# An engine model that lets only one engine at a time use a PSUM tile, other DMA times in it, and a copy placed ahead of two reads

## The chip, the cores and the metric

The kernel runs on one core of one Trainium2 chip. A core has TensorE (matrix products into PSUM, a memory of eight banks), VectorE and ScalarE (both read and write PSUM and SBUF), GpSimd (SBUF alone), and SyncE, which here issues nearly all DMAs. Each engine works through its own queue in order. The metric is the device time of one execution in microseconds; lower is better.

## The reference

One layer of a streaming encoder on 1024 positions of width 2048, in float32. One input projection (2048 to 6752 columns) feeds two mixers side by side. Cut to what matters here:

```python
u = jnp.einsum('bsd,de->bse', h, w_in[layer])
q, k, v, z_attn, q_idx, k_idx, w_idx, z_ssd, xbc, dt_raw = _split_cols(u, IN_WIDTHS)
...
o_attn = _dsa_attention(q, k, v, q_idx, k_idx, w_idx) * jax.nn.silu(z_attn)
o_ssd = _ssd_mixer(xbc, z_ssd, dt_raw, conv_w[layer], conv_b[layer], dt_bias[layer],
                   a_log[layer], d_skip[layer], ssd_norm_w[layer])
mixed = jnp.concatenate([o_attn, o_ssd.astype(o_attn.dtype)], axis=-1)
sub = jnp.einsum('bse,ed->bsd', mixed, w_out[layer])
h = _layer_norm(DEEPNORM_ALPHA * h + sub, ln_g[layer], ln_b[layer])
```

The attention scores all keys with a small indexer, keeps the best 256 for each query and attends to those. The second mixer is the one that the change edits. It splits the sequence into chunks and computes, for each chunk and group of four heads:

```python
xdt = xs * dt[..., None]
a_cum = jnp.cumsum(dt * a, axis=2)
...
cb = jnp.einsum('bclgn,bcsgn->bclsg', cm, bm)
y_diag = jnp.einsum('bclsg,bclsgr,bcsgrp->bclgrp', cb, lmat, xdt)
decay = jnp.exp(a_cum[:, :, -1:] - a_cum)
states = jnp.einsum('bcsgn,bcsgr,bcsgrp->bcgrpn', bm, decay, xdt)
```

The kernel takes chunks of 128 positions where the reference takes 64; the sum is the same.

## The kernel before

**The products.** A float32 product is made of three products of rounded halves: each operand x is split into a high part (xh, wh: a rounded copy, made by ScalarE) and the rest (xl, wl: x minus the high part, made by VectorE or GpSimd), and TensorE adds hi*hi, hi*lo and lo*hi in one PSUM bank. The input projection runs over column tiles of 128 and halves of 512 positions, the output projection over column blocks of 512; both use sums and differences of blocks (a fast matrix product), whose operands are formed by VectorE or GpSimd and partly stored to DRAM and read again. A piece is one weight block of 128 x 1024 and 24 matmuls. Its weight is loaded to wr, split to wh and wl up to two pieces ahead (WAHEAD, L32; w_split, L950), and used. The first product of a pair stays in its PSUM tile (pj); VectorE then adds a reloaded partial result to it (t_u, L740; t_comb, L769), and only after that TensorE adds the next product to the same tile.

**The order of the work.** Nothing is ordered at run time. When the program is built, a planner (class Flow) emits every instruction in an order that it chooses, with the help of a model of the engines (class Sim, L137). The framework then puts in the semaphores that the data need. The planner walks along the pieces of the two projections; between them it looks at a list of tasks, Python generators in order of priority, and lets a task emit its next instructions when it is ready (L444). A task says at each `yield Need(...)` which engines, free buffers and events it needs next. It is ready when its own last instructions, and the events it names, end by the model no later than about the time at which the engine it names gets to them, and when that engine's queue is not over some 2.65 us ahead of TensorE's. An event of a DMA can be given a margin (late). So a figure of the model that is wrong does not make wrong results: it makes a queue in which an instruction stands before its time, and everything behind it on this engine with it, or one that is asked to work later than it could.

**What the model knows.** Sim.run (L257) gives every instruction a start: the later of its engine's clock and the ends of the earlier instructions on which it depends (deps, L164), plus 70 ns between engines. deps goes over the earlier uses of a tile and takes those that overlap in bytes and partitions, one of the two being a write. Two reads of one tile by two engines therefore do not hold each other up in the model. Durations come from formulas (cost, L205). A DMA (L292) takes a lane of eight, its issuing engine's time, then a place on one modelled transfer queue, and lands a fixed time (LAND, L141) after its transfer.

**The mixer's chunk work.** t_ssd (L1971) runs once for each half of the sequence and group, eight times in all, with four chunks each. It starts when the group's convolved inputs lie in DRAM. For each chunk TensorE transposes three blocks of 128 x 128 into one PSUM bank (tag a, of which there are three); VectorE multiplies the first two, 256 columns, by dt (to xdt) and by ddt (to xdd); ScalarE copies the third to bn. The bank is then free for others. After that come the products of the chunk: the masked cb, the chunk's state from bn and xdd, exponentials on ScalarE, the outputs in PSUM tile o, and a gate that needs a small power from GpSimd.

**Names in the profile.** Buffers are shared between purposes, so u is any 128 x 512 buffer in SBUF (bn, xdt and xdd among them; late in the run also xh and xl), s a larger one, a, pj and o PSUM tiles. Every instruction is recorded on one helper line, L318, so groups are told apart by tile and shape. The copy to bn is `ACT u<-a 128x128`, the two reads are `DVE u<-a,dt` and `DVE u<-a,ddt`.

Of the kernel before, what the change touches and what calls it, by code (L numbers as in the profile page):

```python
# [15 lines left out]
D = 2048  # L16
# [108 lines left out]
def in_psum(x):  # L125
    return "PSUM" in str(x.space)


def in_dram(x):
    return "DRAM" in str(x.space)  # L130


def kind_of(x):
    return str(x.dtype).split(".")[-1]


class Sim:  # L137


    LAT = 70.0  # L140
    LAND = 2500.0  # L141

    def __init__(self):
        self.clk = dict(PE=0.0, V=0.0, A=0.0, G=0.0, SP=0.0, AQ=0.0, D=0.0)
# [19 lines left out]
    def deps(self, outs, ins, eng):  # L164
        at, notes = 0.0, []
        for w, xs in ((False, ins), (True, outs)):
            for x in xs:
                k, name, p0, p1, a, b = self.region(x)
                s = self.slot.get(k)
                if s is None:  # L170
                    s = self.slot[k] = [name, 0.0, []]
                elif s[0] != name:
                    s[:] = [name, max([s[1]] + [e[5][0] for e in s[2]]), []]
                at = max(at, s[1])
                for q0, q1, c, d, wr, end, e in s[2]:
                    if (wr or w) and c < b and a < d and q0 < p1 and p0 < q1:
                        if e == eng == "PE":
                            continue
                        at = max(at, end[0] + (0.0 if e == eng else self.LAT))
                notes.append((s, p0, p1, a, b, w))  # L180
        return at, notes
# [23 lines left out]
    def cost(self, eng, op, outs, ins, kw, n):  # L205

        if eng == "PE":
            n = ins[1].free_size()
            if op == "transpose":
                return 111.0, 290.0  # L210
            if kind_of(ins[1]) == "float32":
                if outs[0].partition_size() <= 64:
                    return 153.0, 300.0
                return 2 * max(n / 2.4 + 4, 100.0) if n > 8 else 226.0, max(n / 2.4, 57.0) + 330
            return n / 2.4 + 14.5 if n > 128 else max(n / 2.4 + 4, 80.0), n / 2.4 + 176
        if eng == "V":
            m = max(x.free_size() for x in [*outs, *ins])
            scalar = any(x.free_size() == 1 for x in ins) and n > 1
            if op in ("max", "match_replace"):
                t = (155 if op == "max" else 261) + 1.042 * m  # L220
            elif op == "bn_stats":
                t = 160 + 1.042 * m
            elif op == "stream_shuffle":
                t = 180 + 1.042 * n
            elif op == "tensor_tensor_scan":
                t = 200 + 2.084 * n
            elif op in ("tensor_scalar", "tensor_copy"):
                t = 145 + (1.042 if in_psum(ins[0]) or in_psum(outs[0]) else 0.64) * n + 45 * scalar
            elif op == "reciprocal":
                t = 145 + 5 * n  # L230
            elif op == "tensor_tensor_reduce":
                return 75 + 1.042 * n, 235 + 1.042 * n
            else:
                t = 145 + 1.042 * n + 60 * (op == "scalar_tensor_tensor" and scalar)
            return t - 80, t
        if eng == "A":
            t = (160 if in_psum(ins[0]) else 190) + 0.853 * n + 85 * (len(ins) > 1) + 100 * (len(ins) > 2)
            return (t - 15, t + 90) if len(outs) > 1 else (t - 97, t)
        if op == "memset":
            t = 90 + n  # L240
        elif op == "tensor_tensor":
            t = 180 + 2.16 * n if n > 8 else 600 + 120 * n
        else:
            t = 230 + 0.88 * n
        return t - 30, t
# [46 lines left out]
    def dma(self, eng, out, in_, kw):  # L292
        q = {"SP": "SP", "A": "AQ", "G": "G"}[eng]
        lanes = self.lanes["G" if q == "G" else "H"]
        at, notes = self.deps([out], [in_], "D")
        start = max(self.clk[q], at, lanes.pop(0))
        issue = 1000.0 if eng == "G" else 350.0
        self.clk[q] = start + issue
        sb = in_ if in_dram(out) else out
        row = max(sb.ap[-1][1] * 4, 64)  # L300
        x = max(start + issue, self.clk["D"])
        self.clk["D"] = x + max(out.size(), in_.size()) * 4 * (1 / 360 + 0.6 / row)
        cell = [self.clk["D"] + self.LAND, start, True]
        lanes.append(cell[0])
        self.note(notes, cell, "D")
        return cell
# [282 lines left out]
class Layer:  # L589
# [1381 lines left out]
    def t_ssd(self, h, g):  # L1971
        fl, nc = self.fl, self.nc
# [7 lines left out]
        for cp in range(2):  # L1980
# [10 lines left out]
            bn, xdt, xdd, hs, ea = [fl.new("u", [P, 2, 256]) for _ in range(5)]  # L1991
# [3 lines left out]
            for k, c in enumerate(cs):  # L1995
                yield Need("P", late=2500.0, a=1)
                b = fl.new("a", [P, 512])
                cl = slice(k * P, (k + 1) * P)
                fl.tr(b[:, 0:128], xs[0][:, cl])
                fl.tr(b[:, 128:256], xs[1][:, cl])  # L2000
                fl.tr(b[:, 256:384], bt[:, cl])
                yield Need("VA")
                fl.tt("V", v4(xdt[:, k]), v4(b[:, 0:256]), bc(sd["dt"], c), ALU.mult)
                fl.tt("V", v4(xdd[:, k]), v4(b[:, 0:256]), bc(sd["ddt"], c), ALU.mult)
                fl.act(bn[:, k, 0:128], b[:, 256:384])
                fl.free(b)
            yield Need("P", a=1)
            b = fl.new("a", [P, 256])
# [15 lines left out]
            for k, c in enumerate(cs):  # L2024
# [4 lines left out]
                b = fl.new("a", [P, 256])  # L2029
# [22 lines left out]
            b = fl.new("a", [P, 2, 2, P])  # L2052
# [311 lines left out]
```

## Time and profile before

| | |
|---|---|
| median of 3 runs | 1685.58 us (1684.43 to 1689.02) |
| the profiled execution | 1687.85 us |
| its span, first to last instruction | 1686.0 us |
| mean granted clock of TensorE | 0.984 |
| share of the span, TensorE / VectorE / ScalarE / GpSimd | 97% / 79% / 59% / 12% |
| DMA | 415.53 MB, 246 GB/s on average |

The span is what the profile's rows cover; 1.85 us of the profiled execution lie around it. A row of a timeline has the start, the length, the engine, the instruction with the tile that it writes and the tiles that it reads, the shape, and in brackets how long the engine stood idle just before it and what ended that. TensorE's clock is granted in steps: after a pause it runs at half speed for some microseconds, and a matmul then takes nearly twice as long while it still counts as busy. The busy share alone therefore hides a part of what a pause costs; the granted clock of a window shows it.

### The profile page before, as it was taken

The page shows a single profiled execution, that of the slowest core. Times are in us where ns is not written, and L with a number is a line of the kernel's source. Part 1 is how long each engine was busy: PE and PEld are TensorE (multiplying, and loading weights), DVE is VectorE, ACT ScalarE, POOL GpSimd, SP SyncE. Part 2 cuts the span into 40 slices and gives each one's busy share as a digit, 9 for nine tenths or more (in the row PEclk, how much of TensorE's full clock was granted, in tenths as well). Part 3 has the DMA queues.
Part 4 walks back from the last instruction along what each step waited for, and adds up shares of the span by engine and source line. Part 5 has one row for each costly group of instructions (what it writes and reads, how often), then busy time and mean ns, then how long its engine had stood idle before and what let it go on. Part 6 is the DMA issues. An engine that isn't in the chain of part 4 may idle for free. (4 is left out here: it accounts for less than half of the span.)

```text
span 1686.0 us, 23971 instructions
## 1 busy us (share of the span) xinstructions
PE 1627.5 (97%) x7996; PEld 1346.7 (80%) x7996; DVE 1325.5 (79%) x2430; ACT 993.4 (59%) x1764; POOL 205.2 (12%) x219
## 2 busy tenths in 40 slices
PE   9999999999998999999999999999898999999997
PEld 7787778888886877888888887888677878788885
DVE  5889998998779866787676679867687686749998
ACT  4555666888886788774433556675746555432330
POOL 0000010000000001211123302221011011000110
PEclk9999999999999999999999999999999999999998
DMA  8177575889778867697586685567787999567754
GB/s 305 60 278 250 197 265 188 285 307 348 266 268 279 295 215 264 198 330 250 191 305 227 197 300 162 182 198 250 286 276 278 304 299 319 176 218 261 232 197 153
DMA packets 193211, 415.53 MB, mean 246 GB/s; under 512 B 19776, under 2 KB 56256, under 8 KB 193088
## 3 DMA queue, kind: packets, MB, share of 16 engines
q1 hardware_dynamic: 192656, 413.61, 71.3%
q8 instruction: 63, 1.03, 0.3%
q14 instruction: 60, 0.49, 0.1%
q10 hardware_dynamic: 432, 0.39, 0.1%
HBM read 309.46 MB, written 104.46 MB: 246 GB/s over the span
## 5 line engine op out<-in xcount | busy, mean ns | idle before, releaser
L318 PE MATMUL pj<-xh,wh 128*128 128x512 f32 (+1 forms) x1496 | 586.8, 392 | 15.7 <-DVE u L318 12.3
L318 PE MATMUL pj<-xh,wl 128*128 128x512 f32 (+1 forms) x1496 | 574.8, 384 | 1.8 <-DVE wl L318 1.7
L318 PE MATMUL pj<-xl,wh 128*128 128x512 f32 (+1 forms) x1496 | 574.3, 384 | 0.2 <-DVE xl L318 0.2
L318 DVE TENSOR_TENSOR wl<-wr,wh 128x1024 fp32r<-128x1024 f32 (+2 forms) x232 | 280.4, 1212 | 181.6 <-ACT wh L318 175.4
L318 PEld LDWEIGHTS pj<-xh,wh 128*128 128x128 f32 x1496 | 284.5, 190 | 70.8 <-issue 15.6
L318 ACT ACTIVATE wh<-wr 128x1024 fp32r<-128x1024 f32 (+2 forms) x242 | 248.3, 1031 | 146.5 <-PE pj L318 112.0
L318 PEld LDWEIGHTS pj<-xh,wl 128*128 128x128 f32 x1496 | 284.1, 190 | 60.4 <-DVE wl L318 4.3
L318 PEld LDWEIGHTS pj<-xl,wh 128*128 128x128 f32 x1496 | 284.7, 190 | 50.5 <-DVE xl L318 0.5
L318 PE MATMUL a<-u,u 128*128 128x512 f32 (+3 forms) x734 | 175.1, 359 | 12.1 <-DVE u L318 5.5
L318 PEld LDWEIGHTS a<-u,u 128*128 128x128 f32 x734 | 121.6, 193 | 47.3 <-DVE s L318 18.1
L318 ACT ACTIVATE u<-a 128x512 fp32r<-128x512 f32 (+4 forms) x114 | 53.6, 484 | 154.8 <-PE a L318 67.2
L318 ACT ACTIVATE u<-s,sm 128x640 bf16<-128x640 int16 (+7 forms) x132 | 129.7, 983 | 24.8 <-DVE sm L318 22.8
L318 DVE TENSOR_TENSOR u<-u,u 128x512 f32<-128x512 f32 (+6 forms) x212 | 137.1, 659 | 7.3 <-DMA u<-zs 2.6
L318 PE MATMUL pj<-wh,xh 128*128 128x512 f32 x310 | 126.5, 408 | 0.2 <-DVE u L318 0.2
L318 PE MATMUL pj<-wh,xl 128*128 128x512 f32 x310 | 121.8, 393 | 0.0
L318 PE MATMUL pj<-wl,xh 128*128 128x512 f32 x310 | 121.6, 392 | 0.0
L318 DVE TENSOR_TENSOR u<-pj,u 128x512 f32<-128x512 f32 (+2 forms) x112 | 74.6, 668 | 56.4 <-PE pj L318 55.8
L318 ACT ACTIVATE a<-a 128x512 f32<-128x512 f32 (+3 forms) x160 | 77.0, 505 | 67.6 <-PE a L318 62.0
L318 ACT ACTIVATE u<-u 128x512 f32<-128x512 f32 (+4 forms) x149 | 81.3, 557 | 55.2 <-DVE u L318 48.3
L318 DVE TENSOR_TENSOR wr<-wr,wr 128x1024 f32<-128x1024 f32 (+1 forms) x75 | 92.4, 1233 | 1.3 <-DMA wr<-wt 0.8
L318 DVE SCALAR_TENSOR_TENSOR u<-cv,cw,u 128x512 f32<-128x512 f32 x96 | 72.8, 764 | 9.0 <-POOL cv L318 5.3
L318 POOL TENSOR_SCALAR s<-s,sm 128x640 f32<-128x640 f32 (+7 forms) x64 | 59.7, 949 | 165.1 <-DVE sm L318 126.0
(259 smaller groups left out, 2209.0 us busy)
## 6 DMA issues: line engine op xcount, KB each, us to landing
wr<-wt SPq DMA_DIRECT2D x187, 512.0 KB, 5.5
u<-u SPq DMA_DIRECT2D x110, 256.0 KB, 4.8
wr<-t SPq DMA_DIRECT2D x44, 512.0 KB, 5.4
u<-wo SPq DMA_DIRECT2D x64, 256.0 KB, 4.6
ts<-u SPq DMA_DIRECT2D x64, 256.0 KB, 3.9
wr<-ts SPq DMA_DIRECT2D x32, 512.0 KB, 4.7
s<-xt SPq DMA_DIRECT2D x24, 512.0 KB, 6.2
t<-wr SPq DMA_DIRECT2D x22, 512.0 KB, 4.4
```

Of the source, the lines that this page charges most:

```text
L318: f(*args, **kw)
```

## The change

Four edits, three in the model and one in the mixer.

- In deps any earlier use of a PSUM tile by another engine counts, whether it reads or writes and whichever bytes it touches.
- The DMA model: the issue takes 450 ns where it took 350; the transfer starts 100 ns after the issue starts, where it started after the whole issue; its length is 8.8 ns and 0.0372 ns a byte for each row, over 16 engines, with rows of the shorter side of the two; a load that repeats its source over many partitions (over 300,000 bytes) has a rate of its own; a load lands 2200 ns after its transfer, a store 1600 (STORED), where both took 2500.
- A float32 matmul into at most 64 partitions occupies TensorE for 111 ns where it took 153.
- In t_ssd the copy to bn is asked for and emitted first, by itself; VectorE's two reads come in a step of their own.

The same instructions are emitted as before. Since the planner goes by the model, the order of nearly everything can differ.

```diff
     LAT = 70.0
-    LAND = 2500.0
+    LAND = 2200.0
+    STORED = 1600.0
...
                 k, name, p0, p1, a, b = self.region(x)
+                bank = in_psum(x)
...
                 for q0, q1, c, d, wr, end, e in s[2]:
-                    if (wr or w) and c < b and a < d and q0 < p1 and p0 < q1:
+                    if bank and e != eng or (wr or w) and c < b and a < d and q0 < p1 and p0 < q1:
                         if e == eng == "PE":
                             continue
                         at = max(at, end[0] + (0.0 if e == eng else self.LAT))
...
                 if outs[0].partition_size() <= 64:
-                    return 153.0, 300.0
+                    return 111.0, 300.0
...
-        issue = 1000.0 if eng == "G" else 350.0
+        issue = 1000.0 if eng == "G" else 450.0
         self.clk[q] = start + issue
-        sb = in_ if in_dram(out) else out
-        row = max(sb.ap[-1][1] * 4, 64)
-        x = max(start + issue, self.clk["D"])
-        self.clk["D"] = x + max(out.size(), in_.size()) * 4 * (1 / 360 + 0.6 / row)
-        cell = [self.clk["D"] + self.LAND, start, True]
+        row = min(max(x.ap[-1][1] * 4, 64) for x in (out, in_))
+        x = max(start + 100.0, self.clk["D"])
+        size = max(out.size(), in_.size()) * 4
+        spread = any(s == 0 and n > 1 for s, n in in_.ap) and size > 300000
+        self.clk["D"] = x + (0.0045 * size if spread else size / row * (8.8 + 0.0372 * row) / 16)
+        cell = [self.clk["D"] + (self.STORED if in_dram(out) else self.LAND), start, True]
...
-                yield Need("VA")
+                yield Need("A")
+                fl.act(bn[:, k, 0:128], b[:, 256:384])
+                yield Need("V")
                 fl.tt("V", v4(xdt[:, k]), v4(b[:, 0:256]), bc(sd["dt"], c), ALU.mult)
                 fl.tt("V", v4(xdd[:, k]), v4(b[:, 0:256]), bc(sd["ddt"], c), ALU.mult)
-                fl.act(bn[:, k, 0:128], b[:, 256:384])
                 fl.free(b)
```

## Prediction

> **What bounds the kernel now.** I read the page first: its engine totals say who is short of time.
>
> ```profile
> span 1686.0 us, 23971 instructions
> PE 1627.5 (97%) x7996; PEld 1346.7 (80%) x7996; DVE 1325.5 (79%) x2430; ACT 993.4 (59%) x1764; POOL 205.2 (12%) x219
> ```
>
> TensorE is busy for 1627.5 of 1686.0 us. The change adds and removes no matmul, so all that it can win lies in the other 58.5 us and in the time that TensorE spends at half clock. Next come busy times by stretch (the columns are length, busy time and instructions of each engine, granted clock, DMA share, GB/s). I cut at 570 and 1460 because the state-space mixer's reads of its transposed tiles lie between, by the view of tile ddt (32 instructions; minimum, median, maximum ns; first and last start):
>
> ```profile
> L318 DVE TENSOR_TENSOR u<-a,ddt x26: 406/414/417, 576.6 to 1457.2; 128x256 f32<-128x256 f32 x26
> L318 DVE TENSOR_TENSOR xh<-a,ddt x6: 411/411/414, 1336.8 to 1415.4; 128x256 f32<-128x256 f32 x6
> ```
>
> ```profile
> core 0: us, PE busy (x) PEld busy (x) DVE busy (x) ACT busy (x) POOL busy (x), PEclk, DMA share, GB/s
> 0.00:570.00 570.00, 552.90 (x2593) 450.12 (x2594) 479.84 (x887) 392.41 (x705) 36.77 (x49) 0.99 0.73 259
> 570.00:1460.00 890.00, 860.70 (x4441) 720.82 (x4441) 656.97 (x1258) 536.80 (x974) 147.05 (x154) 0.98 0.74 249
> 1640.00:1686.00 46.00, 34.03 (x151) 27.84 (x149) 41.01 (x67) 0.00 (x0) 3.92 (x4) 0.90 0.49 160
> ```
>
> Without the mixer (0 to 570) TensorE idles 17.1 us and loses 1% of 570, 5.7 us, to the clock: 22.8 us, or 4.0% of the stretch. With the mixer (570 to 1460) it idles 29.3 us and loses 2% of 890, 17.8 us: 47.1 us, or 5.3%. The clock has two digits, so each loss is good to about half a per cent of its stretch. What ends TensorE's idle time in the mixer's stretch, by the waits (total, times, longest):
>
> ```profile
> PE a L318 <- DVE u L318: 9.3, 8, 2.9
> PE a L318 <- ACT u L318: 6.4, 3, 5.0
> PE pj L318 <- DVE u L318: 6.4, 1, 6.4
> PE a L318 <- POOL sm L318: 2.8, 1, 2.8
> ```
>
> Four stalls (6.4, 5.0, 2.9 and 2.8 us) hold 17.1 of the 29.3 us. No row names a DMA. The bound is thus TensorE plus a handful of jams, and the question is what makes the jams.
>
> **Part 1: two engines on one PSUM tile.** In t_ssd a bank takes three transposes; VectorE reads two of them twice (by dt and by ddt) and ScalarE copies the third. The planner of before lets these readers overlap. The groups by form tell what the chip's program does (busy, mean ns, idle before and what ended it):
>
> ```profile
> L318 ACT ACTIVATE u<-a 128x128 f32<-128x128 f32 x26 | 7.2, 275 | 71.4 <-DVE u L318 43.2 <-issue 9.7 <-DMA wr<-wt 6.4
> L318 ACT ACTIVATE xh<-a 128x128 f32<-128x128 f32 x4 | 1.1, 278 | 18.1 <-DVE u L318 18.1
> ```
>
> ScalarE sat idle 43.2 + 18.1 = 61.3 us before 30 copies of 0.28 us, until VectorE was through. The planner sees none of it: it believes ScalarE free, and queues the next weight split behind the copy. The largest such stall, from the timelines of VectorE, ScalarE and TensorE (start, length, idle before):
>
> ```profile
> 1265.91 2.64 DVE L318 TENSOR_TENSOR u<-u 128x256 f32<-128x256 f32 x1
> 1272.24 0.41 DVE L318 TENSOR_TENSOR u<-a,ddt 128x256 f32<-128x256 f32 x1
> 1272.74 0.28 ACT L318 ACTIVATE u<-a 128x128 f32<-128x128 f32 x1 [7.03 <-DVE u L318]
> 1280.45 1.04 ACT L318 ACTIVATE wh<-wr 128x1024 fp32r<-128x1024 f32 x1
> 1281.52 1.23 DVE L318 TENSOR_TENSOR wl<-wr,wh 128x1024 fp32r<-128x1024 f32 x1 [7.94 <-ACT wh L318]
> 1283.50 0.28 ACT L318 ACTIVATE u<-a 128x128 f32<-128x128 f32 x1 [2.02 <-DVE u L318]
> 1283.83 0.58 PE L318 MATMUL a<-u 128*128 128x128 f32 x1 [5.04 <-ACT u L318]
> ```
>
> It is a ring. ScalarE's copy waits 7.03 us for a VectorE that is behind; ScalarE's later work then starts late, the weight's high half (wh) at 1280.45; VectorE waits 7.94 us for wh; its reads for the second chunk come after that, the second copy after those reads, and TensorE, which needs this copy for the chunk's state, stands 5.04 us. The 2.8 us stall has the same root:
>
> ```profile
> 1242.89 0.28 ACT L318 ACTIVATE u<-a 128x128 f32<-128x128 f32 x1 [3.53 <-DVE sm L318]
> 1243.07 1.06 ACT L318 ACTIVATE wh<-wr 128x1024 fp32r<-128x1024 f32 x1
> 1244.20 2.67 POOL L318 TENSOR_TENSOR wl<-wr,wh 128x1024 fp32r<-128x1024 f32 x1 [70.61 <-ACT wh L318]
> 1247.58 1.22 PE L318 MATMUL a<-c,sm 128*128 128x128 f32 x4 [2.78 <-POOL sm L318]
> ```
>
> The copy waits 3.53 us, wh stands behind it, GpSimd's wl behind wh, and the small power that TensorE needs behind wl. Of the 6.4 us stall only a part is of this kind:
>
> ```profile
> 1191.47 0.28 ACT L318 ACTIVATE u<-a 128x128 f32<-128x128 f32 x1 [1.97 <-DVE u L318]
> 1210.62 0.77 PE L318 MATMUL pj<-xh,wh 128*128 128x512 f32 x1 [6.37 <-DVE u L318]
> ```
>
> A stall also costs clock. The windows around three of them and around the 2.9 us one:
>
> ```profile
> 1202.00:1218.00 16.00, 9.63 (x31) 7.44 (x31) 13.63 (x22) 8.66 (x11) 0.00 (x0) 0.79 0.60 212
> 1241.00:1256.00 15.00, 12.22 (x47) 9.80 (x46) 10.46 (x19) 4.21 (x6) 3.77 (x5) 0.77 0.96 312
> 1276.00:1292.00 16.00, 10.96 (x45) 8.82 (x44) 9.66 (x13) 13.72 (x29) 2.44 (x1) 0.79 0.70 242
> 1010.00:1024.00 14.00, 11.08 (x52) 9.38 (x51) 10.32 (x30) 8.47 (x25) 2.26 (x4) 0.88 0.35 117
> ```
>
> 0.21 of 16 us (0.23 of 15) is 3.4 us of full-speed work each, so these stalls are worth 6.2 to 9.8 us; 0.12 of 14 us is 1.7.
>
> The change makes the planner count any use of a PSUM tile by one engine as a bar to the others, and puts the copy first, so that ScalarE waits for the transposes alone. What it adds: VectorE's two reads now wait for the copy, at most 32 x 0.28 = 9.0 us of VectorE with a free ScalarE; behind them on VectorE stand weight splits and sums, which TensorE needs some pieces later. VectorE has 233 us to spare in this stretch, so I cost this at nothing; without that cover, with ScalarE in a run of its own work, it is the second rival. A yield now lies between copy and reads, and the planner queues the reads only when the copy is due. No DMA or queue is moved by hand, though all of them by the new plan.
>
> Size, from both sides. The two stalls told whole are 5.0 + 2.8 + 2 x 3.4 = 14.6 us; with the 6.4 us stall (9.8 with its clock) and the 2.9 us one (4.6 with its clock) the sum is 29.0 us, and that is the upper end. The lower end is none. But the whole order is drawn again, and a new order has jams of its own. So I take the rate: if the mixer's stretch falls to the 4.0% of the stretch without mixer, its loss goes from 47.1 to 890 x 0.040 = 35.6 us. **The gain is 11.5 us**, near what the two whole stalls give.
>
> The Trainium skill, "PSUM — Partial Sum Buffer", section "PSUM bank collisions raise a hardware error", says that no two engines may use one bank in the same quadrant at once, reads against reads included. By it the turn-taking stays and only the waiter changes; the 61.3 us before the copies agree that readers take turns, and what that could do here is the second rival.
>
> **Part 2: transfer times.** The planner's landing of a 512 KB load (128 rows of 4 KB) falls from 350 + 1533 + 2500 = 4383 ns to 100 + 1289 + 2200 = 3589 ns, that of a 256 KB store (rows of 2 KB) from 350 + 805 + 2500 = 3655 to 100 + 680 + 1600 = 2380. The trace has, from the DMA issues and from the view of tile wt (minimum, median, maximum):
>
> ```profile
> wr<-wt SPq DMA_DIRECT2D x187, 512.0 KB, 5.5
> ts<-u SPq DMA_DIRECT2D x64, 256.0 KB, 3.9
> DMA to landing us min/median/max: 3.1/5.5/10.7
> ```
>
> A load's new figure lies 0.5 us above the minimum and 1.9 under the median; the old one lay 1.1 under it. The planner adds queueing of its own, so some of this is made up, but work behind a load will be queued some 0.8 us earlier against the real landing, and an engine may stand at its head. Such waits are rare now:
>
> ```profile
> ACT u L318 <- DMA wr<-wt: 7.5, 2, 6.4
> ACT u L318 <- DMA u<-q: 6.2, 3, 4.8
> ```
>
> Weights are split two pieces ahead, and a piece is 24 matmuls; the chain of waits has their pace.
>
> ```profile
> 1301.38 15.01 PE pj L318 x66
> ```
>
> At 0.227 us each that is 10.9 us of cover, against 0.8. I cost the part at nothing. Where the cover fails, the price is that of the worst stall outside the mixer, with its window:
>
> ```profile
> 514.88 0.77 PE L318 MATMUL pj<-xh,wh 128*128 128x512 f32 x1 [5.96 <-DVE u L318]
> 505.00:521.00 16.00, 10.04 (x35) 7.76 (x34) 14.59 (x22) 10.80 (x21) 1.24 (x2) 0.79 0.92 346
> ```
>
> 6.0 + 3.4 = 9.4 us each. The lower end is a gain of as much, should the new order miss this very stall. The longer SP issue (450 for 350) and the shorter 64-row matmul (111 for 153) change only the plan and belong to the same bounds.
>
> **Sum.** The tail from 1640 has none of this (ScalarE does nothing there): 0. So -11.5 + 0 + 0. The profiled execution took 1687.85 us (span 1686.0 and 1.85 around it), which gives 1676.4; the median of the runs is 1685.58, 2.3 lower, and from it I get **1674.0 us**.
>
> **The rivals.**
>
> 1. *Every jam of this kind goes and nothing takes its place*: 1685.6 - 29.0 = 1656.6. For it: the rings are plain in the trace. Against: a new order has never been free of jams, since 0 to 570 loses 4.0% with no mixer.
> 2. *The wait only changes sides.* ScalarE stays busy for stretches of 7 us (1272.74 to 1280.45 above, wh behind exponentials); a copy queued behind one holds VectorE's reads, as VectorE held the copy. Loss stays 47.1 us: 1685.6, give or take 5.
> 3. *Slower: optimistic landings.* VectorE adds a reloaded partial product to a PSUM tile, in t_u and t_comb, with no margin for the load; TensorE's next product into that tile waits for the sum. If a landing is later than planned by more than VectorE's queue hides, TensorE stands as at 514.88. Two such stalls eat the gain and three turn it round; with four it is 1685.6 - 11.5 + 4 x 9.4 = 1711.7, with three 1702.3, and if the gain in the mixer is none, one is enough: 1695.0. I price it at 1695.0. The Trainium skill, "DMA: Bandwidth & Descriptors", section "Latency and other measured facts", has HBM's access latency at 0.2 us on average and 2 us at high load; by that rule one fixed landing is too early just when queues are full, and the trace's 3.1 to 10.7 us agrees.
>
> **Chances.** Forecast (a gain of 6 to 20 us) 0.50; rival 1, 0.12; rival 2, 0.20; rival 3, 0.18. Measurement tells about 0.3%, 5 us, from no change. So faster 0.62, same 0.20, slower 0.18. The range must take in the forecast's own 1665 to 1680, no change, and most of rivals 1 and 3: 1657 to 1694.
>
> **What would show it.** Right: idle time before the u<-a and xh<-a copies ended by DVE falls from 61 us to under 15; the waits of PE between 570 and 1460 lose the rows on ACT u and POOL sm; the granted clock there rises; PE busy plus the slower clock in 0 to 570 stay within 6 us of 22.8 lost. Rival 2: VectorE's rows of dt and ddt show idle time ended by ACT u. Rival 3: rows "DVE u <- DMA u<-u" of 10 us and more, and a PE stall of 5 us behind one. Wrong altogether: the copies' waits go, and the loss in the mixer's stretch stays, or 0 to 570 loses more by what the other gains.

## The result, and the profile after

The changed kernel takes 1656.04 us (median of 4 runs, 1655.1 to 1659.73) against 1685.74 us before (1684.43 to 1689.02): 29.7 us less, a ratio of 0.9825 with a 95% interval of 0.9805 to 0.9845. The forecast was 1674.0 with a range of 1657 to 1694: the direction is right, the gain is two and a half times what was forecast, and the time lies 1 us outside the range, at the first rival's 1656.6.

The first lines of the page of after:

```profile
span 1654.3 us, 23979 instructions
## 1 busy us (share of the span) xinstructions
PE 1614.9 (98%) x7996; PEld 1337.3 (81%) x7996; DVE 1323.1 (80%) x2429; ACT 1004.6 (61%) x1772; POOL 204.2 (12%) x220
```

The span is 31.7 us shorter. TensorE's idle time went from 58.5 to 1654.3 - 1614.9 = 39.4 us, 19.1 less; the other 12.6 us are in its busy time, with the same 7996 matmuls. The granted clock was 0.984 in that execution of before and 0.995 in this one, so these 12.6 us are time at half clock, and two fifths of the difference between the two executions is clock. Other executions of before had clocks of 0.983 to 0.991 and took 1679.6 to 1691.3 us, so this share is not the same in each. (One more of them, at 1994.4 us with a clock of 0.751, was in a slower state and is left out everywhere.) Where, by the windows of after (columns as before):

```profile
0.00:570.00 570.00, 556.17 (x2607) 451.92 (x2608) 486.75 (x887) 383.12 (x683) 30.02 (x47) 0.99 0.76 268
570.00:1460.00 890.00, 881.73 (x4621) 740.15 (x4620) 664.98 (x1294) 576.16 (x1035) 154.48 (x160) 1.00 0.73 248
1460.00:1640.00 180.00, 174.60 (x762) 143.51 (x761) 161.07 (x233) 45.28 (x55) 18.75 (x12) 0.99 0.67 224
```

The mixer's stretch idles 8.3 us where it idled 29.3, at a granted clock of 1.00 where it had 0.98. It gets 180 more matmuls done in the same 890 us. The stretch without mixer loses 13.8 us idle and 1% of clock: 19.5 us, where it lost 22.8. What TensorE still waits for in the mixer's stretch, by the waits of after:

```profile
PE a L321 <- DVE sm L321: 2.1, 4, 0.8
PE pj L321 <- ACT u L321: 1.8, 1, 1.8
PE a L321 <- POOL u L321: 1.7, 2, 1.1
PE a L321 <- DVE u L321: 1.5, 3, 0.7
```

All four big stalls are gone; the longest wait in this stretch is 1.8 us. (Behind it, between 1460 and 1640, stands one of 4.7 us on DVE xh.) And the copies, in the groups by form, with the idle time before VectorE's reads of dt from their tile view behind them:

```profile
L321 ACT ACTIVATE u<-a 128x128 f32<-128x128 f32 x32 | 8.5, 269 | 17.9 <-PE a L321 17.7
```

```profile
its engine sat idle before it (us, times) until:
  ACT u L321: 3.7, 1
```

No copy waits for VectorE any more; where ScalarE idles before one, it waits for the transposes. VectorE has paid 3.7 us, in one wait.

This agrees with the ring, but a trace of another order cannot prove it: every queue differs from before. That is what the experiments are for.

### The profile page after: what moved, and what is told of

It is laid out like the page before. It is cut to its first block, busy times and chain, and to the rows that moved or that the text cites. A ratio compares the mean times of both kernels' runs of the same rounds, so it can differ in the third digit from the quotient of the medians.

```text
span 1654.3 us, 23979 instructions
## 1 busy us (share of the span) xinstructions
PE 1614.9 (98%) x7996; PEld 1337.3 (81%) x7996; DVE 1323.1 (80%) x2429; ACT 1004.6 (61%) x1772; POOL 204.2 (12%) x220
## 4 chain that ended last, share of the span: by engine, by line
PE 48%; DVE 13%; ACT 12%; DMA 7%; issue 4%; POOL 0%; SPq 0%; DVEq 0%; ACTq 0%; POOLq 0%
PE pj L321 37%; PE a L321 9%; ACT u L321 8%; DVE u L321 6%; DVE wl L321 3%; PE o L321 2%; ACT wh L321 2%; DMA wr<-wt 2%; DVE xl L321 2%; DVE xh L321 1%; DVE wr L321 1%; ACT s L321 1%; DVE s L321 1%; ACT L321 1%; DMA u<-xn 1%
## 5 line engine op out<-in xcount | busy, mean ns | idle before, releaser
L321 PE MATMUL a<-u,u 128*128 128x512 f32 (+3 forms) x744 | 177.5, 356 | 12.6 <-DVE s L321 5.3
L321 PEld LDWEIGHTS a<-u,u 128*128 128x128 f32 x744 | 120.5, 189 | 52.4 <-DVE s L321 20.4
L321 DVE TENSOR_TENSOR u<-u,u 128x512 f32<-128x512 f32 (+7 forms) x202 | 127.7, 642 | 21.4 <-DMA u<-wo 5.9
L321 ACT ACTIVATE u<-s,sm 128x896 bf16<-128x896 int16 (+7 forms) x132 | 129.5, 982 | 16.6 <-DVE sm L321 14.7
L321 DVE TENSOR_TENSOR wr<-wr,wr 128x1024 f32<-128x1024 f32 (+1 forms) x79 | 97.3, 1233 | 4.1 <-DMA wr<-wt 3.4
L321 POOL TENSOR_SCALAR s<-s,sm 128x640 f32<-128x640 f32 (+7 forms) x64 | 63.2, 1002 | 125.9 <-DVE sm L321 89.2
L321 DVE SCALAR_TENSOR_TENSOR s<-a,wsc,s 128x512 f32<-128x512 f32 (+3 forms) x120 | 73.2, 644 | 6.4 <-ACT a L321 4.3
```

The costliest lines, as they stand in the source:

```text
L321: f(*args, **kw)
```

## The experiments

Three theories: **the ring** (the direction of the wait between the copy and the reads makes the jams), **the draw** (any new order is faster or slower by chance, and this one was lucky), and **the transfer times** (better landings make a better order). Times of before differ a little between the groups of runs, from 1684.3 to 1686.4 us; each ratio is against before on the same chip.

### The wait turned round, all queues kept

The planner of before does not see the wait between two readers. So the copy can be written ahead of the reads in the same step without moving anything in its plan: all five engines get the same instructions in the same order, and only the direction of the wait changes.

```diff
                 yield Need("VA")
+                fl.act(bn[:, k, 0:128], b[:, 256:384])
                 fl.tt("V", v4(xdt[:, k]), v4(b[:, 0:256]), bc(sd["dt"], c), ALU.mult)
                 fl.tt("V", v4(xdd[:, k]), v4(b[:, 0:256]), bc(sd["ddt"], c), ALU.mult)
-                fl.act(bn[:, k, 0:128], b[:, 256:384])
```

> The kernel before with the copy to bn written ahead of VectorE's two reads inside the same step; the planner's model and the order of every engine's queue stay those of before, only the direction of the wait turns. Ring theory (ScalarE's copies waiting for VectorE make the mixer's jams): the idle time before the u<-a and xh<-a copies ended by DVE falls from 61 us to under 5, the 5.0 and 2.8 us stalls go, 1665 to 1673 us. New-order theory (the gain is the draw of another order): nothing moves, 1683 to 1688. Transfer-time theory (the better landings order the work better): 1683 to 1688.

Measured: **1656.65 us**, ratio 0.9834 (0.9813 to 0.9855). The swap, one line moved in the order of before, is worth 28.5 us, nearly the whole gain. The ring theory's range of 1665 to 1673 was missed by 8 us, on the fast side: it priced little more than the two stalls that had been told whole. The page of this run, its copies by form, and its mixer's stretch:

```profile
span 1654.6 us, 23984 instructions
## 1 busy us (share of the span) xinstructions
PE 1614.6 (98%) x7996; PEld 1339.0 (81%) x7996; DVE 1323.3 (80%) x2430; ACT 995.3 (60%) x1764; POOL 205.9 (12%) x219
```

```profile
L318 ACT ACTIVATE u<-a 128x128 f32<-128x128 f32 x26 | 7.0, 267 | 20.3 <-PE a L318 20.1
...
L318 ACT ACTIVATE xh<-a 128x128 f32<-128x128 f32 x4 | 1.1, 272 | 12.2 <-PE a L318 12.2
```

```profile
570.00:1460.00 890.00, 878.42 (x4606) 739.39 (x4605) 675.72 (x1292) 553.94 (x1001) 152.03 (x159) 1.00 0.75 253
```

The idle time that DVE ended, 61.3 us, is gone; TensorE idles 11.6 us instead of 29.3, and the clock stands at 1.00. Here is the pair of copies that made the worst ring before, in this run's timelines of ScalarE and VectorE (in each fence the copies, then the reads):

```profile
1249.24 0.26 ACT L318 ACTIVATE u<-a 128x128 f32<-128x128 f32 x1
...
1258.31 0.26 ACT L318 ACTIVATE u<-a 128x128 f32<-128x128 f32 x1
```

```profile
1255.45 0.41 DVE L318 TENSOR_TENSOR u<-a,dt 128x256 f32<-128x256 f32 x1
...
1259.58 0.42 DVE L318 TENSOR_TENSOR u<-a,dt 128x256 f32<-128x256 f32 x1
```

VectorE is as late as ever: its first read comes 6.2 us after the copy. But nobody waits for it. Neither copy has a bracket, ScalarE goes on to its table and its exponentials, and no TensorE stall follows. Since TensorE's queue is the same in both kernels, the very matmuls that stood 2.92, 2.78, 5.04 and 2.25 us in before can be looked up here. They have no bracket (the first is one of the five of its row):

```profile
1006.56 0.67 PE L318 MATMUL a<-u,u 128*128 128x128 f32 x5
1233.95 0.61 PE L318 MATMUL a<-c,sm 128*128 128x128 f32 x4
1261.52 0.49 PE L318 MATMUL a<-u 128*128 128x128 f32 x3
1406.56 0.39 PE L318 MATMUL a<-o,u 128*128 128x1 f32 x3
```

The last of these stood, in before, at a stall that the prediction did not list:

```profile
1434.72 0.98 PE L318 MATMUL a<-o,u 128*128 128x1 f32 x4 [2.25 <-DVE u L318]
```

What VectorE pays for the turned wait is in the view of tile dt:

```profile
  ACT u L318: 10.3, 6
```

10.3 us against 61.3 us. The Trainium skill's rule cited in the prediction ("PSUM — Partial Sum Buffer", section "PSUM bank collisions raise a hardware error") agrees with this run: the readers still take turns, and the waiter is now VectorE, for 10.3 us. What two reads at once would do, no run here shows. The cost hardly reaches TensorE. The 6.4 us stall, of which the prediction gave the ring only a part, is still there, at the same matmul, with 5.5 us:

```profile
1199.97 0.76 PE L318 MATMUL pj<-xh,wh 128*128 128x512 f32 x1 [5.50 <-DVE u L318]
```

### The same turn in three other orders

The mirror: the plan of after, with the real copy issued behind the reads. TensorE's, VectorE's, GpSimd's and SyncE's queues keep their order; ScalarE's differs in seven places.

```diff
                 yield Need("A")
-                fl.act(bn[:, k, 0:128], b[:, 256:384])
+                fl.placed(fl.sim.run("A", "activation", [bn[:, k, 0:128]], [b[:, 256:384]], {"func": AF.Copy}))
                 yield Need("V")
                 fl.tt("V", v4(xdt[:, k]), v4(b[:, 0:256]), bc(sd["dt"], c), ALU.mult)
                 fl.tt("V", v4(xdd[:, k]), v4(b[:, 0:256]), bc(sd["ddt"], c), ALU.mult)
+                nc.scalar.engine.activation(bn[:, k, 0:128], b[:, 256:384], AF.Copy)
```

> The kernel after with its plan kept, but the copy to bn issued behind VectorE's two reads, so that it waits for them as before. The queues of TensorE, VectorE, GpSimd and SyncE keep the order of after; ScalarE's differs in seven places, where the copy stands some instructions later. Ring theory: the copies wait 50 us or more for DVE again and TensorE stalls in the mixer's stretch, 1666 to 1686 us. Draw theory (the wait costs only in unlucky orders, and after has a lucky one): 1656 to 1662.

Measured: 1673.27 us, 0.9925 (0.9903 to 0.9947): 17.2 us slower than after. Copies by form, the mixer's window, and the first waits of TensorE in it:

```profile
L2010 ACT ACTIVATE u<-a 128x128 f32<-128x128 f32 x32 | 8.9, 277 | 85.4 <-DVE u L321 69.6 <-DVE xh L321 5.8 <-PE pj L321 5.1
```

```profile
570.00:1460.00 890.00, 867.18 (x4504) 725.32 (x4503) 653.03 (x1274) 565.82 (x1021) 154.96 (x159) 0.99 0.73 245
```

```profile
PE a L321 <- DVE u L321: 6.9, 8, 2.1
PE a L321 <- POOL u L321: 3.8, 2, 2.3
PE pj L321 <- ACT u L321: 3.7, 1, 3.7
```

The copies wait 75.4 us for VectorE again, and TensorE's idle time in the stretch goes from 8.3 to 22.8 us with a lower clock.

A third order is that of the new DMA model alone (its run is below, 1675.11 us), a fourth that of before planned with 80 ns between engines instead of 70 (1674.01 us, below). In both the swap of the first experiment keeps every queue.

> The kernel before with the new DMA model (1675.1 us alone) and the copy written ahead of the reads in the same step; every queue has the order of the run with the DMA model alone. Ring theory: the 81 us of copies' waits by DVE go and with them 10 to 25 us, 1650 to 1665. Draw theory: within 5 us of 1675.

Measured: 1662.67 us, 0.988 (0.9848 to 0.9912), 12.4 us less than 1675.11.

> The kernel before with 80 ns between engines (1674.0 us) and the copy written ahead of the reads in the same step; every queue keeps its order. Ring theory: the copies' 72 us of waits by DVE go and 8 to 22 us with them, 1652 to 1666. Draw theory: within 4 us of 1674.

Measured: 1654.49 us, 0.9811 (0.9789 to 0.9834), 19.5 us less than 1674.01. In both the copies wait no longer for VectorE. The orders with the DMA model, first the old and then the turned wait, and then those with 80 ns:

```profile
L320 ACT ACTIVATE u<-a 128x128 f32<-128x128 f32 x30 | 8.3, 275 | 80.4 <-DVE u L320 77.7 <-PE pj L320 2.7
...
L320 ACT ACTIVATE u<-a 128x128 f32<-128x128 f32 x30 | 7.8, 268 | 25.6 <-PE a L320 25.6
...
L318 ACT ACTIVATE u<-a 128x128 f32<-128x128 f32 x30 | 8.3, 275 | 77.6 <-DVE u L318 56.2 <-DVE xl L318 9.5 <-issue 5.9
...
L318 ACT ACTIVATE u<-a 128x128 f32<-128x128 f32 x30 | 8.0, 268 | 18.0 <-PE a L318 15.9 <-DMA wr<-ts 2.1
```

So the turned wait alone is worth 28.5, 17.2, 12.4 and 19.5 us in four orders: 19 on average. By the ratios, each against before on its own chip, it is 28.0, 16.9, 9.4 and 19.6; the third is the least certain, to some 7 us. **The ring is shown**: the wait of the copies for the reads costs time in every order in which it was turned, and its price depends on the order it sits in. With the DMA model alone the copies waited longest, yet the turn brought least. An idle sum of an engine thus says that there is something to win, and not how much. What sets the price is in part the clock: see the last section.

### Each part alone

Copy first as in the change (a step of its own), with the model of before; then the rule in deps alone; then the DMA model alone, all as the change's diff has them.

> The kernel before with the t_ssd edit alone (copy first, in a step of its own); model of before. Ring theory: 1655 to 1670 us, the loss of the mixer's stretch under 30 us. New-order theory: anywhere from 1670 to 1700. Transfer-time theory: 1680 to 1690.

> The kernel before with the rule in deps alone (any use of a PSUM tile by another engine counts); the copy still comes after the reads, but the planner knows that it waits. Ring theory: the planner puts other ScalarE work ahead of the copy, so a part of the gain, 1662 to 1678 us. New-order theory: 1670 to 1700. Transfer-time theory: 1680 to 1690.

> The kernel before with the DMA model of after alone. Ring theory: the copies still wait some 60 us for DVE and the mixer's stretch still loses 40 us or more, 1678 to 1696 us. New-order theory: 1670 to 1700. Transfer-time theory: 1660 to 1675.

Measured: 1688.62 us (1.002, 1.0005 to 1.0036), 1686.22 (1.0007, 0.9994 to 1.0021) and 1675.11 (0.9936, 0.9913 to 0.996). None of the three fell into the ring theory's range. The second was to gain a part, 1662 to 1678, and gained nothing; the third, with its copies waiting, came out 3 us faster than the 1678 that was its lower end, and just past the 1675 that was the transfer-time theory's upper one. The first, which was to give 1655 to 1670, was the plainest miss: with the copies first as in the swap, and no copy waiting for VectorE, it gains nothing. The windows of that run show why:

```profile
570.00:1460.00 890.00, 876.37 (x4564) 736.90 (x4563) 667.92 (x1272) 554.26 (x993) 152.65 (x163) 0.99 0.75 255
1460.00:1640.00 180.00, 158.51 (x707) 129.73 (x706) 145.76 (x215) 54.06 (x74) 13.20 (x9) 0.94 0.66 219
```

The mixer's stretch idles 13.6 us instead of 29.3, as it should. The loss is new, and lies behind it: 21.5 us idle, where before had 0.2. The clock of 0.94 must not be added to that as 6% of 180 us, because most of the half-clock time fell into the pause itself, where TensorE had nothing to do:

```profile
1577.50:1591.00 13.50, 0.00 (x0) 0.00 (x0) 11.50 (x18) 0.63 (x1) 0.00 (x0) 0.50 1.01 318
```

From the timelines of GpSimd, VectorE, SyncE and TensorE:

```profile
1555.52 0.69 POOL L318 TENSOR_TENSOR sm<-sm,mhalf 128x2 f32<-128x2 f32 x1 [99.76 <-DVE sm L318]
1566.39 0.86 DVE L318 SCALAR_TENSOR_TENSOR u<-u,dn,a 128x256 f32<-128x256 f32 x2
1567.28 0.38 SPq L318 DMA_DIRECT2D my<-u  x1
1591.02 0.79 PE L318 MATMUL pj<-wh,xh 128*128 128x512 f32 x1 [17.40 <-ACT xh L318]
```

The mixer's last gate takes its power at 1556 us; GpSimd had been idle for 99.8 us before it. The gate's block is stored at 1567, loaded again, split, and TensorE stands 17.4 us for it. The rule alone has the same late jam, 15.8 us, and so has the kernel after with the old DMA model (next), 14.8 us. From the waits of TensorE between 1460 and 1640, of the run with the rule alone:

```profile
PE pj L319 <- ACT xh L319: 15.8, 2, 9.3
```

With the rule alone the planner knows of the copies' wait and still lets them wait 73 us; in that order, knowing it brought no gain. The 111 ns for small matmuls was never run by itself.

### The change less one part

> The kernel after with the DMA model of before. Ring theory: copies without waits, mixer's stretch losing under 20 us, 1655 to 1665. Transfer-time theory (the new figures are what keeps the late gates from a jam near 1575): the stall of 10 us or more of PE on ACT xh near 1575 is back, 1670 to 1692. Draw theory: either.

> The kernel after without the rule in deps: copy first, new DMA model, 111 ns. Ring theory: 1655 to 1665, since the copy has no reader ahead of it whether the planner knows the rule or not. If the rule itself orders the work better: 1668 to 1690 with copies' waits by DVE still near none. Draw theory: either.

> The kernel after with the copy behind the two reads in the plan too: rule, new DMA model, 111 ns. Ring theory: copies wait 50 us or more for DVE, the planner allows for it in part, 1662 to 1678. If the planner's knowledge is enough: 1655 to 1661. Draw theory: either.

These are the change's diff without the part named. Measured: 1663.91 us (0.9867, 0.9848 to 0.9885) without the DMA model, 1652.21 (0.9808, 0.9781 to 0.9835) without the rule, 1659.86 (0.984, 0.9817 to 0.9862) with the copy last but planned for. No one part is needed for most of the gain. Without the DMA model the late jam is back, as the transfer-time theory said, and the time is in the ring theory's range all the same. Without the rule the kernel is the fastest run of the study, 3.8 us under after, though the two intervals overlap, and 3 us under the ring theory's range.

The last was a miss for the ring theory, which had 1662 to 1678. It fell into the rival range, 1655 to 1661, for a planner whose knowledge of the wait is enough. Its copies wait for VectorE 72.5 us in all, more than in before; TensorE's idle time in the mixer's stretch is 13.8 us, and it gains 26 us. So turning the wait is one way to the gain and not the only one: an order can also keep these waits and miss the jams. Whether the rule in the planner found that order or chance did is open, since the rule alone gained nothing.

### The starved gate

Why is one gate 100 us late? A gate is a task of priority 2. A task is ready only when its engine's queue is at most 2.65 us ahead of TensorE's, but tasks of priority 0 may go 5.3 us ahead. Once the output projection has begun, priority-0 work keeps VectorE's queue above 2.65 us, and a gate that comes then finds no room: by the planner's log of that order, once this gate's own data are there it is refused for VectorE's queue alone. With the gates at priority 0, and the copy first under the old model:

```diff
-                fl.add(self.t_gate(h, g, (cp,)), 2, f"gate{h}{g}")
+                fl.add(self.t_gate(h, g, (cp,)), 0, f"gate{h}{g}")
```

(and so at the other three places that add a gate).

> Copy first with the model of before (1688.6 us before this), and the gates' tasks at priority 0 instead of 2. Starved-gate theory (a last gate that misses its place waits some 100 us behind VectorE's priority-0 work, and its block then stops TensorE near 1575): the sixteenth gate's power on GpSimd moves from 1556 to under 1480 us, the stalls of 17.4 and 2.5 us go, 1652 to 1668 us. Bad-draw theory (an order under the old transfer times is just worse): 1678 to 1692.

Measured: 1658.13 us (0.9846, 0.9816 to 0.9877), 30.5 us less than 1688.62. The last gate's power and the stretch behind the mixer:

```profile
1481.70 0.69 POOL L318 TENSOR_TENSOR sm<-sm,mhalf 128x2 f32<-128x2 f32 x1 [39.22 <-DVE sm L318]
```

```profile
1460.00:1640.00 180.00, 178.06 (x802) 146.91 (x802) 165.41 (x248) 46.07 (x57) 12.25 (x11) 1.00 0.68 228
```

1482 instead of 1556 us, and 1.9 us idle instead of 21.5 (the expectation's bound of 1480 was missed by 2 us). Of the 30.5 us, 19.6 are the idle time behind the mixer that is gone; the rest lies elsewhere in what is again a new order. The starved gate had eaten the copy's gain. Then the same under the new transfer times without the rule, and with the whole change:

> Copy first, new DMA model, 111 ns, no rule in deps (1652.2 us), with the gates at priority 0. If the transfer times help only by keeping the last gate from starving, this equals the run with copy first, old DMA model and gates at priority 0 (1658.1) within 8 us, 1650 to 1663. If they help by themselves: 1640 to 1648.

> The kernel after with the gates at priority 0. After has no starved gate, so only a new draw: 1648 to 1668.

Measured: 1655.05 us (0.9813, 0.9775 to 0.9851) and 1660.88 (0.9858, 0.982 to 0.9896). The first lies 3.1 us under the 1658.13 of the same kernel with the old transfer times (and the old cost of 64-row matmuls). By the ratios it is 5.6 us. That is less than what draws alone do, below: once no gate starves, the transfer times show no gain of their own. The second is 4.8 us slower than after, and no more than a new draw was expected of it.

### How far a draw goes

Planner before and planner after, with 60 and 80 ns for the delay between engines instead of 70, and nothing else:

```diff
-    LAT = 70.0
+    LAT = 60.0
```

> The kernel before with the planner's delay between engines at 60 ns instead of 70: a new draw and nothing else. It shows how far a draw alone moves the time. Ring theory: the mixer's stretch still loses 25 us or more, 1672 to 1700. If a draw alone can do what the change did: below 1665.

> The kernel before with 80 ns for the planner's delay between engines: a second draw of the planner before, 1675 to 1695, with copies waiting 50 us or more for DVE.

> The kernel after with the planner's delay between engines at 60 ns instead of 70: a new draw of the changed planner. Ring theory: 1648 to 1668, copies without waits for DVE. If after is a lucky draw: 1670 to 1690.

> The kernel after with 80 ns for the planner's delay between engines: a second draw of the changed planner, 1650 to 1670; below 1650 or above 1672 would make the draw as large as the change.

| delay in the planner | before | after |
|---|---|---|
| 70 ns (the kernels themselves) | 1685.74 | 1656.04 |
| 60 ns | 1679.07 | 1666.43 |
| 80 ns | 1674.01 | 1668.27 |
| mean | 1679.6 | 1663.6 |

Draws of one planner lie 12 us apart. Before was the worst of its three, after the best of its three. The means differ by 16.0 us, so about half of the 29.7 is the change in general, and the rest is an unlucky order before and a lucky one after. With three draws each this split is rough: by their scatter the 16.0 is uncertain by some 14 us either way. That the turned wait helps rests on the four pairs with equal or nearly equal queues, and not on these means. Before with 80 ns came out 1 us under the range expected of it, 1675 to 1695. The 1668.27 has the starved gate again, under the new transfer times, so these do not prevent it. Its wait, and the gate's late store by SyncE:

```profile
PE pj L321 <- ACT xh L321: 18.2, 1, 18.2
```

```profile
1540.89 0.38 SPq L321 DMA_DIRECT2D my<-xl  x1
```

> The kernel after with 80 ns between engines (1668.3 us, one stall of 18.2 us on ACT xh) and the gates at priority 0. Starved-gate theory: that stall goes, 1645 to 1660. Otherwise 1664 to 1672.

Measured: 1657.75 us (0.9834, 0.9809 to 0.9859): the stall on ACT xh is gone, and the time is 10.5 us less. That stall was the starved gate; 10.5 us is not its exact price, because the new priority draws a new order, with a stall of 6.0 us of another kind in the same stretch.

## Why the prediction was right and where it failed

**The bound and the ring: right.** TensorE plus a handful of jams, the jams on ACT u and POOL sm, the copies' waits: the swap in the order of before shows that the ring made three of the four; the 6.4 us stall stays with 5.5. The prediction's first mark (61 us to under 15) came out at none, the rows on POOL sm and the large one on ACT u are gone, the clock rose from 0.98 to 1.00, and the stretch without mixer stayed within 6 us of its 22.8.

**The sum: the term of the newly drawn order was mis-sized.** The step that failed is "So I take the rate: if the mixer's stretch falls to the 4.0% of the stretch without mixer". It fell to 0.9% idle with no loss of clock that two digits show: read as the prediction reads it, from 47.1 to 8.3 us in after, a term of 38.8 where the sum has 11.5. (Behind the mixer, from 1460 to 1640, after loses 7.2 us read in the same way, where before was busy for 179.82 of 180 us at a clock of 1.00.) The loss before the mixer was taken for a background that any order has, and it is not one: 9.4 of its 22.8 us are the single stall at 514.88, by the prediction's own price. The mixer's stretch has no such floor. In all thirteen profiled kernels whose copies come first it idles 8.3 to 20.4 us, 0.9 to 2.3%, at a clock of 0.99 or 1.00. The 11.5 us should have been near the upper end that was worked out by the four stalls one by one, 29.0; the swap, which draws no new order at all, measured 28.5. That near match flatters the sum: the largest of the four stalls stayed with 5.5 us, so part of the 28.5 came from smaller waits that were not in it, such as the 2.25 us at 1434.72, whose window (1426 to 1442) had a clock of 0.79 too. The prices of the stalls also count a little twice, as do the 47.1 us: time at half clock was priced as lost work even where TensorE stood idle in it. In the 5.0 us stall these are 2.9 us:

```profile
1280.90:1283.80 2.90, 0.00 (x0) 0.00 (x0) 2.22 (x4) 0.89 (x3) 0.00 (x0) 0.51 0.98 287
```

So its clock cost 3.4 - 1.4 = 2.0 us, and not 3.4. And the sum itself gives 1674.1, not 1674.0.

What the prediction feared of a new draw is real, though not there: it came behind the mixer, as the starved gate, and in after it did not occur.

**Part 2, transfer times at nothing: not contradicted.** The new model alone gave 10.1 us against before on its chip (1685.17), which is within the 12 us that draws of one planner differ by. With the gates in their place the old and the new times came out 3.1 us apart. The reason given, that 10.9 us of cover stand against 0.8 us of earlier landings, was not tested by a run of its own.

**The rivals.** The first named the time, 1656.6, and had 0.12; its clause "nothing takes its place" was the right description of the mixer's stretch. The second, that the wait only changes sides, fell: it changes sides and costs VectorE 3.7 us (10.3 in the swap), which TensorE hardly sees. The third, optimistic landings, shows as more waits of VectorE on DMAs, some 20 us in all where before had 6, but small ones, by the waits of after:

```profile
DVE u L321 <- DMA u<-wo: 5.9, 7, 1.9
...
DVE u L321 <- DMA u<-u: 0.7, 1, 0.7
```

The mark for it was a row on DMA u<-u of 10 us and more; it has 0.7. The rule of the Trainium skill behind this rival ("DMA: Bandwidth & Descriptors", section "Latency and other measured facts") is not refuted, since landings still spread, from 3.2 to 9.5 us for the weight loads of after; how much of that spread is latency and how much queueing, and that it reaches TensorE by this way, no run here shows.

**The range** ended at 1657 because the first rival was given only in part. With 29.0 us worked out as an upper end, the range had to reach it whole, and a few us beyond for draws of 12 us.

## What to carry to other kernels

Where two engines read one PSUM tile, let the one go first whose queue is short, or whose late work holds up the other: look for an engine that idles before short copies "until" a busy engine, and turn the wait. Here that won 12 to 28 us of some 1680 in four orders. When an order is made by a planner, separate the edit from the new draw: try the edit in the old order if that can be done, and give each planner two or three neutral draws before a gain of one per cent is believed. Here a stall priced from its own rows, with its clock, was a better guide than a rate taken from another stage, though partly by luck. Time at half clock costs only where the engine works in it: two of the windows above, at 0.50 and 0.51, hold no matmul at all.

## What was not expected of the hardware

Of the 31.4 us by which the span of the swapped kernel is shorter, only 18.5 us (58.5 to 40.0) are idle time of TensorE; 12.9 us (1627.5 to 1614.6 of busy time, for the same matmuls) are clock. The granted clock rose from 0.984 to 0.993, which is 15.4 us of full speed (1686.0 x 0.016 less 1654.6 x 0.007), a part of it while TensorE stood idle.

This is no fixed rate. In the order with the DMA model the swap shortened the span by 13.4 us, of which 8.6 are idle time, and the clock was 0.994 with and without it. In the order with 80 ns it was 23.0 us with 15.1 of idle time, and the clock went from 0.993 to 0.995. So the turn brought most in the order whose stalls had cost the most clock, with windows at 0.77 to 0.88. In the two others busy time fell as well: by 4.8 us with no change of clock, and by 7.9 us, of which the clock is at most 3.5 (1673.4 x 0.007 less 1650.4 x 0.005). What the rest was stays open.
